# Feature transform with 256-column matmuls, and the rest queries as one weight block ahead of the small transpose

## The chip, the core and the metric

The kernel runs on one core of one Trainium2 chip. The metric is device time in microseconds (us) of one execution; the time of a kernel is the median of its runs. A profiled execution gives the trace, and its own time is used where rows of the trace are added up.

## What is computed

Two layers of an encoder over 1040 positions (16 learned meta tokens and 1024 inputs) with 1024 channels. Each layer reads one RMS-normed input through a combined projection, and three groups of heads work on its parts. Cut to what the change touches:

```python
def fourier_mix(f_in, fourier_w):          # 4 heads of 64 channels
    y = fft2(x, axes=(position, channel), norm="ortho").real
    return einsum('blhc,hcd->blhd', y, fourier_w)

def attend(qb):                            # 4 heads, 128 nope + 64 rope channels
    s = einsum('bqhd,bkhd->bhqk', qb, k) * scale
    return einsum('bhqk,bkhd->bqhd', softmax(s), v)

h = h + concat[fourier * silu(g_f), pool * silu(g_p), attention * silu(g_a)] @ w_out[l]
```

All arithmetic is to float32 accuracy: an operand is split into a rounded high part and a low part that holds the difference (`hilo`, L75: ScalarE writes the high part, VectorE subtracts), and a product takes three matmuls, high by high, high by low and low by high (`mm3`, L70).

## The kernel before, in words

The program is written stage by stage for TensorE, and a scheduler fixes the order of the instructions on each engine when the program is built. Each engine then works its own list in that order and waits where a buffer or an operand is not ready. Tiles come from pools with a fixed number of buffers: `slab` (36 buffers of 128x1056, SBUF), `mid` (10 buffers, SBUF), and in PSUM six banks with tag `mm` and two with tag `t`. A new tile takes a buffer as soon as the last reader of the tile that held it is done; until then its first writer waits, and with it all that stands behind that writer on its engine.

**Fourier group** (`dft_z` L498, `dft_y` L541, four passes `ty` per layer in the order 0, 2, 1, 3, between the matmuls of the gate projection of the attention group). `mc` holds the feature transform joined with `fourier_w`: four 128x128 matrices (cosine or sine, channel block j), each as a high and a low part. In `dft_z`, a row block `c` of the folded input (two full blocks; in every second pass a third of 80 rows, `fr`, that POOL puts together) is the stationary operand and `mc` streams past it. For each j there is one `mm3` of 128 columns into a `t` bank (L529), so six matmuls for a row block: `ah` by `mc` high, `ah` by `mc` low, `al` by `mc` high. ScalarE and VectorE then split the bank into `zt` (L532) or `ze` (L536, L537). `dft_y` takes `zt` as weights and streams the sine and cosine tables `dt` (262 columns), which POOL's queue loads into `mid` buffers (L506, L508).

**Attention** (L888 to L922). There are 16 groups `gi` per layer (4 heads by 4 blocks of 256 queries). A group has two tiles of 128 queries; `scores` (L705) fills three `mm` banks of 348, 348 and 344 keys, VectorE takes their maxima (L718), ScalarE the exponentials with a sum (L765, `soft` L760), VectorE scales (L773). `transposes` (L776) of the group before turns the probabilities for `values` (L811): steps kp 0 to 3 are four full transposes into a `t` bank (L802), then split by `hilo` into `pth` and `ptl`; step kp 4 is the small transpose of the last 16 keys (`rm`, L784), split into `pr`. `values` runs one group later still, into one `mm` bank (24 matmuls of 256 columns and two short ones).

**Rest queries.** In layer 0 the 1040 queries leave 16 over. `scores_rest` (L723) takes the 16 of all four heads as 64 rows: POOL writes their high parts, low parts and rope parts into `q3h` and `q3l`, blocks of 64 columns with zeros elsewhere (L725 to L732). For each of three key ranges 14 matmuls fill 64 rows of a bank: an `mm3` for each head and two for rope (L739 to L741). VectorE takes the maximum from PSUM (L742), and `soft` reads the bank. This is called in group 2, after `transposes(prev, (2, 3, 4))` and after `soft` of the second tile (L911 to L915).

Of the kernel before, what the change touches and what calls it, by code (L numbers as in the profile page):

```python
# [21 lines left out]
HEADS = 4  # L22
# [10 lines left out]
def fp(ap):  # L33
    return ap.bitcast(F32)
# [3 lines left out]
def hymba_encoder(ctx: ExitStack, tc: tile.TileContext, ht, win, wkr, vecs, fw, pw, wuq, wuk, wuv,  # L38
                  wout, cos_t, sin_t, dft_t, feat_t, fix_t, out):
    nc = tc.nc  # L40
# [23 lines left out]
    def bank(tag="mm"):  # L64
        return psum.tile([P, 512], F32, tag=tag, name=nm(tag), bufs=NMM if tag == "mm" else 8 - NMM)

    def mm(o, a, b, first, last):
        nc.tensor.matmul(o, a, b, start=first, stop=last)  # L68

    def mm3(o, wh, wl, xh, xl, first, last):  # L70
        mm(o, wh, xh, first, False)
        mm(o, wh, xl, False, False)
        mm(o, wl, xh, False, last)

    def hilo(hi, lo, src):  # L75
        nc.scalar.copy(hi, src)  # L76
        nc.vector.tensor_tensor(lo, src, fp(hi), ALU.subtract)  # L77
# [135 lines left out]
    for i in range(2):  # L213
        kind, src, k, m = jobs[i]
# [12 lines left out]
    for k in range(KC):  # L227
        h = slab("h")
# [36 lines left out]
    for l in range(DEPTH):  # L265
# [66 lines left out]
        s = add_square(add_square(None, zk[0], L), zk[1], L)  # L332
# [147 lines left out]
        nc.sync.dma_start(fwr, fw[l].rearrange("j p c -> p j c"))  # L480
        feat = mid("feat", [P, 2, P], F32)
        nc.sync.dma_start(feat, feat_t)
        mc = slab("mc", F32R, (P, 2, 4, P))
        b = bank("t")
        for part in range(2):
            for j in range(2):
                nc.tensor.matmul(b[:, (2 * part + j) * P:(2 * part + j + 1) * P], feat[:, part, :], fwr[:, j, :],
                                 start=True, stop=True)
        hilo(mc[:, 0], mc[:, 1], b.rearrange("p (a c) -> p a c", a=4))
        del fwr, feat  # L490
        FG.append(tile_now(scaled_tile(CQ, off, fn=AF.Silu)))
        Y = [slab("y0"), slab("y1")]
# [5 lines left out]
        def dft_z(ty):  # L498
            tabs, zs = [], []
            for c in range(3):  # L500
                rows = slice(0, P if c < 2 else 80)
                t = mid("dt", [P, 2, NF])
                if l == 0 and ty == 0:
                    nc.gpsimd.tensor_copy(t[rows, 0, 0:1], er[rows, 0:1])
                if c < 2:
                    nc.gpsimd.dma_start(t, dft_t[ty, c])  # L506
                else:
                    nc.gpsimd.dma_start(t[rows, 0, :], dft_t[ty, c, 0:80, 0, :])  # L508
                tabs.append(t)
            kind = ty // 2  # L510
            if ty % 2 == 0:
                fr = mid("fr", [P, 2, 2, 80])
                nc.gpsimd.memset(fp(fr), 0.0)
                for j in range(2):
                    for i in range(2):
                        for r in (0, 32, 64):
                            nc.gpsimd.tensor_copy(fr[:, j, i, r:r + 10].rearrange("p (a c) -> p a c", a=2),
                                                  fp(FH[j][i][:, ty:ty + 2, 256:261]))
            for c in range(2 + (ty % 2 == 0)):
                m = P if c < 2 else 80  # L520
                b = bank("t")
                for j in range(2):
                    if c < 2:
                        r = slice(P * c, P * c + P)
                        ah, al = FH[j][0][:, ty, r], FH[j][1][:, ty, r]
                    else:
                        ah, al = fr[:, j, 0, :], fr[:, j, 1, :]
                    mi = 2 * kind + j
                    mm3(b[0:m, j * P:(j + 1) * P], ah, al, mc[:, 0, mi, :], mc[:, 1, mi, :], True, True)  # L529
                if c < 2:  # L530
                    z = mid("zt", [P, 2, 256])
                    hilo(z[:, 0, :], z[:, 1, :], b[:, 0:256])  # L532
                    zs.append(z)
                else:
                    z = mid("ze", [80, 256])
                    nc.scalar.copy(z, b[0:80, 0:256])  # L536
                    nc.vector.tensor_tensor(z[32:64, :], b[32:64, 0:256], fp(z[32:64, :]), ALU.subtract)  # L537
                    ends[kind] = z
            return tabs, zs

        def dft_y(ty, tz, cc):  # L541
# [43 lines left out]
        zq, s = [], None  # L585
        for t in range(3):
            z = tile_now(raw_tile(CQ, off))
            s = add_square(s, z, NQ)
# [4 lines left out]
            if t == 1:  # L593
                KRH, KRL = slab("krh", F32R), slab("krl", F32R)
# [59 lines left out]
        parts = []  # L654
# [65 lines left out]
            nc.vector.tensor_reduce(mx[:, 3:4], mx[:, 0:3], AX.X, ALU.max, negate=True)  # L720
            return P, mx, bs

        def scores_rest():  # L723

            q3h, q3l = mid("q3h", [P, 5, 64]), mid("q3l", [P, 4, 64])  # L725
            nc.gpsimd.memset(fp(q3h), 0.0)
            nc.gpsimd.memset(fp(q3l), 0.0)
            for h in range(HEADS):
                r = slice(16 * h, 16 * h + 16)
                nc.gpsimd.tensor_copy(q3h[:, h, r], fp(QN[h][0][:, 1024:1040]))  # L730
                nc.gpsimd.tensor_copy(q3l[:, h, r], fp(QN[h][1][:, 1024:1040]))
                nc.gpsimd.tensor_copy(q3h[:, 4, r], fp(QR[h][:, 1024:1040]))  # L732
            mx = small("mx", [P, 4])
            bs = []
            for i, (c0, n) in enumerate(FULL):
                ks = slice(c0, c0 + n)
                o = bank()[0:64, :n]
                for h in range(HEADS):
                    mm3(o, q3h[:, h, :], q3l[:, h, :], KN[h][0][:, ks], KN[h][1][:, ks], h == 0, False)  # L739
                mm(o, q3h[:, 4, :], KRH[:, ks], False, False)  # L740
                mm(o, q3h[:, 4, :], KRL[:, ks], False, True)  # L741
                nc.vector.tensor_reduce(mx[0:64, i:i + 1], o, AX.X, ALU.max)  # L742
                bs.append(o)
            nc.vector.tensor_reduce(mx[0:64, 3:4], mx[0:64, 0:3], AX.X, ALU.max, negate=True)
            return 64, mx, bs

        def transposes_rest(p):
            t3 = sm_pool.tile([P, 2, 8, 64], F32R, tag="t3", name=nm("t3"), bufs=1)
# [9 lines left out]
            return t3, r3  # L758

        def soft(sc, rem=None):  # L760
            m, mx, bs = sc
            p = slab("p")
            sums = small("sums", [P, 4])
            for i, (c0, n) in enumerate(FULL):
                nc.scalar.activation(p[0:m, c0:c0 + n], bs[i], AF.Exp, bias=mx[0:m, 3:4],  # L765
                                     accum_out=sums[0:m, i:i + 1])
            nc.vector.tensor_reduce(sums[0:m, 3:4], sums[0:m, 0:3], AX.X, ALU.add)
            nc.vector.reciprocal(sums[0:m, 3:4], sums[0:m, 3:4])
            if rem is None:
                nc.vector.tensor_scalar(p[0:m, :L], p[0:m, :L], sums[0:m, 3:4], None, ALU.mult)  # L770
            else:
                nc.scalar.activation(rem, p[:, 1024:1040], AF.Copy, scale=sums[:, 3:4])
                nc.vector.tensor_scalar(p[:, :1024], p[:, :1024], sums[:, 3:4], None, ALU.mult)  # L773
            return p
# [114 lines left out]
        for gi, (h, g, tiles) in enumerate(groups):  # L889
            if g == 0:  # L890
                gate[h] = slab("gate")
                nc.sync.dma_start(gate[h][:, :NQ], gate_d[l][h, :, :NQ])
            cur = (h, g, small("rm", [P, 32], 3), [], [None] * 5)
            sc = scores(h, tiles[0])
            if gi == 0:
                cur[3].append(soft(sc, cur[2][:, 0:16]))
                QN.append(nope(CQN, 3, CQ, "qn"))
            if pend is not None:
                values(pend)
                if pend[1] == 3:  # L900
                    gate.pop(pend[0])
            if gi > 0:
                cur[3].append(soft(sc, cur[2][:, 0:16]))
            if prev is not None:
                transposes(prev, (0, 1))
            sc = scores(h, tiles[1])
            if gi == 0:
                QN.append(nope(CQN, 3, CQ, "qn"))
                del CQN
            if prev is not None:  # L910
                transposes(prev, (2, 3, 4))  # L911
                prev[3].clear()
            cur[3].append(soft(sc, cur[2][:, 16:32]))
            if l == 0 and gi == 2:
                rest = soft(scores_rest())  # L915
# [165 lines left out]
```

## Time and profile before

| what | value |
|---|---|
| median of 3 runs | 1073.85 us (1073.82 to 1075.18) |
| the profiled execution | 1075.23 us |
| its span, first to last instruction | 1073.5 us |
| TensorE (PE) busy | 1054.4 us, 98%, 6774 matmuls |
| TensorE weight loads (PEld) | 998.4 us, 93% |
| VectorE (DVE) busy | 700.0 us, 65% |
| ScalarE (ACT) busy | 512.8 us, 48% |
| GpSimd (POOL) busy | 96.1 us, 9% |
| mean granted clock of TensorE | 0.995 |

Matmuls are pipelined: a row of 0.32 us is the latency of one, and the next one starts well before it ends. What a matmul costs in a stream is the distance from its start to the start of the next. A bracket at the end of a row of a timeline is the idle time of the engine before that instruction, and what ended it.

### The profile page before, as it was taken

How to read it: one execution, taken by the hardware profiler on the slowest of the kernel's cores; microseconds unless marked ns; L12 is line 12 of the kernel's file. 1: busy time of each engine (PE TensorE's matmuls, PEld its weight loads, DVE VectorE, ACT ScalarE, POOL GpSimd, SP SyncE). 2: the span in 40 equal slices, each digit the busy share in tenths (PEclk: the TensorE clock that was granted, in tenths of full speed). 3: DMA queues.
4: the chain of work that ended last, by engine and by line, in shares of the span. 5: the costliest groups of instructions: out<-in, count | busy, mean ns of one | idle time of the engine just before them, and what ended most of it. 6: DMA issues, size and time to landing. Idle time of an engine off the chain costs nothing.

```text
span 1073.5 us, 17783 instructions
## 1 busy us (share of the span) xinstructions
PE 1054.4 (98%) x6774; PEld 998.4 (93%) x6774; DVE 700.0 (65%) x1422; ACT 512.8 (48%) x1203; POOL 96.1 (9%) x223
## 2 busy tenths in 40 slices
PE   8999999999999999999999999999999999999996
PEld 7999999999998899999999898888888899999995
DVE  6677543547577588888645765334575678888755
ACT  7532232353155467677534312323431566777674
POOL 0100020000000000001430001210000000000055
PEclk9999999999999999999999999999999999999998
DMA  6331123126550000013644111241274500001513
GB/s 234 93 120 40 49 84 116 51 73 228 196 144 1 21 17 5 22 40 119 195 133 118 51 49 40 83 125 45 84 261 156 128 1 21 21 20 41 168 40 118
DMA packets 52373, 95.26 MB, mean 89 GB/s; under 512 B 5312, under 2 KB 27584, under 8 KB 52288
## 3 DMA queue, kind: packets, MB, share of 16 engines
q1 hardware_dynamic: 49216, 89.17, 25.5%
q0 software_dynamic: 3072, 4.96, 1.9%
q8 instruction: 53, 0.87, 0.3%
q14 instruction: 32, 0.26, 0.1%
HBM read 66.62 MB, written 21.14 MB: 82 GB/s over the span
## 4 chain that ended last, share of the span: by engine, by line
PE 91%; DVE 4%; DMA 2%; ACT 1%; issue 1%; SPq 0%; DVEq 0%; ACTq 0%
PE mm L68 85%; PE t L802 4%; PE t L68 2%; DVE mx L718 1%; DMA pwr<-in_pw 1%; ACT p L765 1%; DVE ptl L77 1%; DMA h<-in_ht 1%; DVE wp L77 0%; DMA hq<-part_d 0%; DVE p L773 0%; DVE om L829 0%; PE t L784 0%; DMA wraw<-in_win 0%; DVE wlo L77 0%
## 5 line engine op out<-in xcount | busy, mean ns | idle before, releaser
L68 PE MATMUL mm<-hh,whi 128*128 128x348 f32 (+2 forms) x728 | 246.0, 340 | 1.3 <-ACT hh L202 0.7
L68 PE MATMUL mm<-hl,whi 128*128 128x348 f32 (+2 forms) x728 | 245.7, 339 | 0.4 <-DVE hl L203 0.4
L68 PE MATMUL mm<-hh,wlo 128*128 128x348 f32 (+2 forms) x728 | 245.9, 339 | 0.2 <-DVE wlo L77 0.2
L76 ACT CAST whi<-wraw 128x512 fp32r<-128x512 f32 (+3 forms) x110 | 64.5, 586 | 239.5 <-PE mm L68 233.1
L77 DVE TENSOR_TENSOR wlo<-wraw,whi 128x512 fp32r<-128x512 f32 (+3 forms) x110 | 70.8, 646 | 131.0 <-PE mm L68 77.8
L68 PEld LDWEIGHTS mm<-hh,whi 128*128 128x128 f32 x728 | 136.5, 188 | 9.6 <-ACT hh L202 1.3
L68 PEld LDWEIGHTS mm<-hl,whi 128*128 128x128 f32 x728 | 136.8, 188 | 8.3 <-DVE hl L203 0.7
L68 PEld LDWEIGHTS mm<-hh,wlo 128*128 128x128 f32 x728 | 136.8, 188 | 7.6 <-DVE wlo L77 0.5
L765 ACT ACTIVATE p<-mm,mx 128x348 f32<-128x348 f32 (+2 forms) x195 | 105.6, 555 | 13.3 <-DVE mx L720 12.7
L68 PE MATMUL mm<-pth,v 128*128 128x256 f32 (+1 forms) x512 | 106.6, 284 | 1.8 <-ACT p L765 0.8
L76 ACT CAST pth<-t 128x512 fp32r<-128x512 f32 x128 | 75.8, 593 | 67.8 <-PE t L802 67.2
L718 DVE TENSOR_REDUCE mx<-mm 128x1 f32<-128x348 f32 (+1 forms) x192 | 95.5, 513 | 15.4 <-PE mm L68 14.7
L68 PE MATMUL mm<-mah,wp 128*128 128x256 f32 (+1 forms) x512 | 94.1, 283 | 0.0
L77 DVE TENSOR_TENSOR ptl<-t,pth 128x512 fp32r<-128x512 f32 x128 | 86.3, 684 | 8.4 <-ACT pth L76 7.4
L68 PEld LDWEIGHTS mm<-pth,v 128*128 128x128 f32 x512 | 83.2, 189 | 3.4 <-ACT pth L76 1.2
L68 PEld LDWEIGHTS mm<-mah,wp 128*128 128x128 f32 x512 | 79.6, 189 | 0.1
L68 PE MATMUL mm<-ptl,v 128*128 128x256 f32 (+1 forms) x256 | 78.9, 308 | 0.0
L802 PE MATMUL t<-ident,p 128*128 128x128 f32 x512 | 76.8, 275 | 0.5 <-DVE ptl L77 0.2
L68 PE MATMUL mm<-mal,wp 128*128 128x256 f32 (+1 forms) x256 | 72.6, 284 | 0.0
L868 POOL TENSOR_TENSOR ssq<-ssq,sq 128x256 f32<-128x256 f32 (+1 forms) x49 | 37.6, 768 | 346.1 <-ACT sq L863 344.1
L68 PE MATMUL mm<-knh,qnh 128*128 128x348 f32 (+1 forms) x192 | 66.0, 344 | 0.5
L68 PE MATMUL mm<-knl,qnh 128*128 128x348 f32 (+1 forms) x192 | 61.9, 322 | 0.0
(237 smaller groups left out, 2190.7 us busy)
## 6 DMA issues: line engine op xcount, KB each, us to landing
wraw<-in_win SPq DMA_DIRECT2D x66, 256.0 KB, 2.6
wraw<-in_wout SPq DMA_DIRECT2D x32, 256.0 KB, 2.8
hq<-part_d SPq DMA_DIRECT2D x12, 512.0 KB, 5.4
dt<-in_dft_t POOLq DMA_DIRECT2D x16, 262.0 KB, 3.1
hres<-in_ht SPq DMA_DIRECT2D x8, 520.0 KB, 6.5
part_d<-hres SPq DMA_DIRECT2D x8, 520.0 KB, 3.7
hres<-h_d SPq DMA_DIRECT2D x8, 512.0 KB, 6.4
part_d<-hres SPq DMA_DIRECT2D x8, 512.0 KB, 3.9
```

Source lines behind the costliest of these rows:

```text
L68: nc.tensor.matmul(o, a, b, start=first, stop=last)
L76: nc.scalar.copy(hi, src)
L77: nc.vector.tensor_tensor(lo, src, fp(hi), ALU.subtract)
L718: nc.vector.tensor_reduce(mx[:, i:i + 1], o, AX.X, ALU.max)
L765: nc.scalar.activation(p[0:m, c0:c0 + n], bs[i], AF.Exp, bias=mx[0:m, 3:4], accum_out=sums[0:m, i:i + 1])
L802: nc.tensor.transpose(bv[:, a, t * P:(t + 1) * P], ps[t][:, kc * P:(kc + 1) * P], ident)
L868: eng.tensor_tensor(ssn[:, cs_], ssn[:, cs_], q[:, :n], ALU.add)
```

## The change

It has two parts. In the feature transform, `mc` is laid out with the high and the low part of each matrix side by side, so that `ah` meets both in one matmul of 256 columns; `al` meets the high part alone in one of 128. A bank then holds the main sum in one half of each j and the product with the low part in the other half, and they are added when the bank is read: ScalarE copies the main sum rounded (high part), VectorE subtracts it from the main sum into a new `mid` tile `zd`, and VectorE adds the other half into the low part. That is one instruction and one `mid` tile more for each row block.

For the rest queries, `q3` holds the high and the low parts of a head as one weight block of 128 columns (64 and 64). A key range takes four matmuls with that block against the high keys (128 output rows), four of 64 rows against the low keys and two for rope: ten in place of fourteen. ScalarE copies rows 64 to 127 to a slab `s3`, VectorE adds rows 0 to 63, and VectorE takes the maximum from `s3`; the exponentials are then written in place. The blocks are built in group 0 (`rest_parts`), and in group 2 the scores of the rest come after `soft` of the second tile and ahead of the small transpose (kp 4).

```diff
-        mc = slab("mc", F32R, (P, 2, 4, P))
+        mc = slab("mc", F32R, (P, 4, 2, P))
...
-        hilo(mc[:, 0], mc[:, 1], b.rearrange("p (a c) -> p a c", a=4))
+        hilo(mc[:, :, 0, :], mc[:, :, 1, :], b.rearrange("p (a c) -> p a c", a=4))
...
                     mi = 2 * kind + j
-                    mm3(b[0:m, j * P:(j + 1) * P], ah, al, mc[:, 0, mi, :], mc[:, 1, mi, :], True, True)
+                    r = slice(256 * j, 256 * j + 256)
+                    mm(b[0:m, r], ah, mc[:, mi, :, :].rearrange("p a c -> p (a c)"), True, False)
+                    mm(b[0:m, 256 * j:256 * j + P], al, mc[:, mi, 0, :], False, True)
+                bv = b.rearrange("p (j a c) -> p a j c", j=2, a=2)
                 if c < 2:
                     z = mid("zt", [P, 2, 256])
-                    hilo(z[:, 0, :], z[:, 1, :], b[:, 0:256])
                     zs.append(z)
+                    hi, lo, rows = z[:, 0, :], z[:, 1, :], slice(0, P)
                 else:
                     z = mid("ze", [80, 256])
-                    nc.scalar.copy(z, b[0:80, 0:256])
-                    nc.vector.tensor_tensor(z[32:64, :], b[32:64, 0:256], fp(z[32:64, :]), ALU.subtract)
                     ends[kind] = z
+                    hi, lo, rows = z, z[32:64, :], slice(32, 64)
...
+                own = hi[rows]
+                nc.scalar.copy(hi, bv[0:m, 0])
+                d = mid("zd", [P, 2, P], F32)[rows]
+                nc.vector.tensor_tensor(d, bv[rows, 0], fp(own), ALU.subtract)
+                nc.vector.tensor_tensor(lo, bv[rows, 1], d, ALU.add)
...
-        def scores_rest():
+        def rest_parts():
+            q3, qr3 = mid("q3", [P, 4, P]), mid("qr3", [P, 64])
+            nc.gpsimd.memset(fp(q3), 0.0)
             for h in range(HEADS):
                 r = slice(16 * h, 16 * h + 16)
+                nc.gpsimd.tensor_copy(q3[:, h, 16 * h:16 * h + 16], fp(QN[h][0][:, 1024:1040]))
+                nc.gpsimd.tensor_copy(q3[:, h, 64 + 16 * h:80 + 16 * h], fp(QN[h][1][:, 1024:1040]))
+                nc.gpsimd.tensor_copy(qr3[:, r], fp(QR[h][:, 1024:1040]))
+            return q3, qr3
+
+        def scores_rest(parts):
...
+            s3, bs = slab("s3"), []
             for i, (c0, n) in enumerate(FULL):
                 ks = slice(c0, c0 + n)
-                o = bank()[0:64, :n]
+                b = bank()
+                o, s = b[0:64, :n], s3[0:64, ks]
                 for h in range(HEADS):
-                    mm3(o, q3h[:, h, :], q3l[:, h, :], KN[h][0][:, ks], KN[h][1][:, ks], h == 0, False)
-                mm(o, q3h[:, 4, :], KRH[:, ks], False, False)
-                mm(o, q3h[:, 4, :], KRL[:, ks], False, True)
-                nc.vector.tensor_reduce(mx[0:64, i:i + 1], o, AX.X, ALU.max)
-                bs.append(o)
+                    if h == 0:
+                        mm(b[:, :n], q3[:, h, :], KN[h][0][:, ks], True, False)
+                    mm(o, q3[:, h, 0:64], KN[h][1][:, ks], False, False)
+                mm(o, qr3, KRH[:, ks], False, False)
+                mm(o, qr3, KRL[:, ks], False, False)
+                for h in range(1, HEADS):
+                    mm(b[:, :n], q3[:, h, :], KN[h][0][:, ks], False, h == HEADS - 1)
+                nc.scalar.copy(s, b[64:128, :n])
+                nc.vector.tensor_tensor(s, o, s, ALU.add)
+                nc.vector.tensor_reduce(mx[0:64, i:i + 1], s, AX.X, ALU.max)
+                bs.append(s)
...
             if prev is not None:
-                transposes(prev, (2, 3, 4))
+                transposes(prev, (2, 3))
+            if l == 0 and gi == 2:
+                cur[3].append(soft(sc, cur[2][:, 16:32]))
+                sc = scores_rest(rest)
+                transposes(prev, (4,))
+                rest = soft(sc)
+            else:
...
```

How the built lists of the engines stand to each other: outside the four passes of the Fourier group (both layers) and groups 2 to 6 of layer 0's attention, TensorE's list is the same in both programs.

**TensorE, one row block of the feature transform in layer 0** (`t_` is the bank, `fah` and `fal` the input's parts, two numbers for j = 0 and 1). Before, ended by the next matmul of the projection:

```order
L68 MATMUL t_1585<-mc_1292,fah_1269 128x128 x2
L68 MATMUL t_1585<-mc_1292,fal_1270 128x128
L68 MATMUL t_1585<-mc_1292,fah_1284 128x128 x2
L68 MATMUL t_1585<-mc_1292,fal_1285 128x128
L68 MATMUL mm_1615<-hh_131,whi_1453 128x348
```

With the change:

```order
L68 MATMUL t_1585<-mc_1292,fah_1269 128x256
L68 MATMUL t_1585<-mc_1292,fal_1270 128x128
L68 MATMUL t_1585<-mc_1292,fah_1284 128x256
L68 MATMUL t_1585<-mc_1292,fal_1285 128x128
L68 MATMUL mm_1615<-hl_150,whi_1453 128x348
```

Six matmuls became four, each with a weight load of its own; the place among the projection's matmuls moved by a few.

**TensorE, group 2 of layer 0, from the last full transposes on** (`mm_3650`, `mm_3666` and `mm_3682` are the banks of the rest's three key ranges, `mm_3709` is the next group's scores). Before:

```order
L802 MATMUL t_3609<-ident,p_3410 128x128
L802 MATMUL t_3609<-ident,p_3484 128x128
L784 MATMUL t_3618<-ident,rm_3386 32x128
L68 MATMUL mm_3650<-knh_2314,q3h_3633 64x348
L68 MATMUL mm_3650<-knl_2315,q3h_3633 64x348
L68 MATMUL mm_3666<-knh_2314,q3h_3633 64x348
L68 MATMUL mm_3666<-knl_2315,q3h_3633 64x348
L68 MATMUL mm_3682<-knh_2314,q3h_3633 64x344
L68 MATMUL mm_3682<-knl_2315,q3h_3633 64x344
L68 MATMUL mm_3709<-knh_2314,qnh_3155 128x348
```

With the change, the first key range (bank `mm_3644`; the other two follow, with the same ten):

```order
L824 MATMUL t_3624<-ident,p_3425 128x128
L824 MATMUL t_3624<-ident,p_3499 128x128
L68 MATMUL mm_3644<-knh_2314,q_549_3377 128x348
L68 MATMUL mm_3644<-knl_2315,q_549_3377 64x348
L68 MATMUL mm_3644<-knl_2350,q_549_3377 64x348
L68 MATMUL mm_3644<-knl_2385,q_549_3377 64x348
L68 MATMUL mm_3644<-knl_2420,q_549_3377 64x348
L68 MATMUL mm_3644<-krh_2216,qr_550_3378 64x348
L68 MATMUL mm_3644<-krl_2217,qr_550_3378 64x348
L68 MATMUL mm_3644<-knh_2349,q_549_3377 128x348
L68 MATMUL mm_3644<-knh_2384,q_549_3377 128x348
L68 MATMUL mm_3644<-knh_2419,q_549_3377 128x348
```

and further on, behind all thirty of them:

```order
L68 MATMUL mm_3672<-knh_2419,q_549_3377 128x344
L68 MATMUL mm_3702<-knh_2314,qnh_3155 128x348
L68 MATMUL mm_3702<-knl_2315,qnh_3155 128x348
L68 MATMUL mm_3702<-knh_2314,qnl_3156 128x348
L68 MATMUL mm_3702<-krh_2216,qr_3002 128x348
L68 MATMUL mm_3702<-krl_2217,qr_3002 128x348
L68 MATMUL mm_3709<-knh_2314,qnh_3155 128x348
L806 MATMUL t_3687<-ident,rm_3401 32x128
L68 MATMUL mm_3709<-knl_2315,qnh_3155 128x348
```

The small transpose stood right behind the eight full ones; it now stands behind thirty matmuls of the rest and six of the next scores. Before, all but six matmuls of the rest came after the fifteen of the next scores.

**VectorE, the row blocks of the first pass.** Before:

```order
L299 TENSOR_TENSOR u_1396<-mm_1450,y_384 128x348
L77 TENSOR_TENSOR zt_1427<-t_1420,zt_1427 128x256
L77 TENSOR_TENSOR zt_1437<-t_1430,zt_1437 128x256
L299 TENSOR_TENSOR u_1396<-mm_1451,y_384 128x348
L537 TENSOR_TENSOR ze_1447<-t_1440,ze_1447 32x256
```

With the change:

```order
L299 TENSOR_TENSOR u_1396<-mm_1450,y_384 128x348
L547 TENSOR_TENSOR zd_1427<-t_1420,zt_1425 128x256
L547 TENSOR_TENSOR zd_1437<-t_1430,zt_1435 128x256
L548 TENSOR_TENSOR zt_1425<-t_1420,zd_1427 128x256
L548 TENSOR_TENSOR zt_1435<-t_1430,zd_1437 128x256
L299 TENSOR_TENSOR u_1396<-mm_1451,y_384 128x348
```

Each row block has a second instruction on VectorE (20 in both layers), and the bank is free after the second.

## Rows read from the trace of the kernel before

**Rows 1.** The page: busy us (share of the span) and instructions by engine.
```profile
PE 1054.4 (98%) x6774; PEld 998.4 (93%) x6774; DVE 700.0 (65%) x1422; ACT 512.8 (48%) x1203; POOL 96.1 (9%) x223
```

**Rows 2.** Waits of PE: engine and line waited for, us in total, times, longest.
```profile
PE t L784 <- DVE ptl L77: 2.7, 2, 2.3
```

**Rows 3.** Timeline of PE, layer 0, group 2: start us, us, what, count.
```profile
345.44 1.10 PE L802 MATMUL t<-ident,p 128*128 128x128 f32 x8
348.85 0.28 PE L784 MATMUL t<-ident,rm 128*32 128x128 f32 x1 [2.31 <-DVE ptl L77]
...
349.29 0.49 PE L68 MATMUL mm<-knh,q3h 128*64 128x348 f32 x1
...
352.48 0.42 PE L68 MATMUL mm<-knh,qnl 128*128 128x348 f32 x1
352.73 0.32 PE L68 MATMUL mm<-krh,qr 128*128 128x348 f32 x1
352.89 0.32 PE L68 MATMUL mm<-krl,qr 128*128 128x348 f32 x1
```

**Rows 4.** Timelines of ACT and of DVE in group 2.
```profile
349.14 0.63 ACT L76 CAST pth<-t 128x512 fp32r<-128x512 f32 x1
...
348.11 0.69 DVE L77 TENSOR_TENSOR ptl<-t,pth 128x512 fp32r<-128x512 f32 x1
...
350.26 0.69 DVE L77 TENSOR_TENSOR ptl<-t,pth 128x512 fp32r<-128x512 f32 x1
```

**Rows 5.** Window: from:to us, length, busy of PE, PEld, DVE, ACT, POOL; PEclk, DMA.
```profile
348.95:352.48 3.53, 3.53 (x15) 3.28 (x15) 1.96 (x5) 1.42 (x7) 0.00 (x0) 0.54 0.00 0
```

**Rows 6.** Timeline of PE, one row block of the feature transform.
```profile
150.49 0.33 PE L68 MATMUL t<-mc,fah 128*128 128x128 f32 x2
150.66 0.27 PE L68 MATMUL t<-mc,fal 128*128 128x128 f32 x1
150.77 0.39 PE L68 MATMUL t<-mc,fah 128*128 128x128 f32 x2
...
151.10 0.37 PE L68 MATMUL mm<-hh,whi 128*128 128x348 f32 x1
```

**Rows 7.** Timeline of PE, table matmuls and a row block of 80.
```profile
148.08 0.52 PE L68 MATMUL mm<-dt,zt 128*128 128x262 f32 x3
148.44 0.58 PE L68 MATMUL t<-mc,fr 128*80 128x128 f32 x6
148.86 0.46 PE L68 MATMUL mm<-dt,zt 128*128 128x262 f32 x2
```

**Rows 8.** Groups of PE by form: count, busy us, mean ns, idle before.
```profile
L68 PE MATMUL t<-mc,fah 128*128 128x128 f32 x64 | 10.9, 264 | 0.0
```

**Rows 9.** Tile `t` in layer 0's four passes, and a window there.
```profile
L77 DVE TENSOR_TENSOR zt<-t,zt x8: 414/424/425, 145.1 to 182.3; 128x256 fp32r<-128x256 f32 x8
...
166.00:171.00 5.00, 5.00 (x37) 5.00 (x36) 3.67 (x10) 2.71 (x6) 0.55 (x1) 1.00 0.49 139
```

**Rows 10.** DMA issues: KB each, median us to landing.
```profile
dt<-in_dft_t POOLq DMA_DIRECT2D x16, 262.0 KB, 3.1
```

**Rows 11.** Timeline of PE, eight transposes with no wait behind them.
```profile
399.21 1.12 PE L802 MATMUL t<-ident,p 128*128 128x128 f32 x8
400.08 0.41 PE L68 MATMUL mm<-knh,qnh 128*128 128x348 f32 x1
```

**Rows 12.** Timeline of ACT, group 2, the first tile's first exponential.
```profile
345.31 0.56 ACT L765 ACTIVATE p<-mm,mx 128x348 f32<-128x348 f32 x1
```

**Rows 13.** Timeline of PE, the values of the group behind the rest.
```profile
359.51 1.04 PE L802 MATMUL t<-ident,p 128*128 128x128 f32 x8
361.37 0.39 PE L68 MATMUL mm<-pth,v 128*128 128x256 f32 x1 [0.83 <-ACT p L765]
```

**Rows 14.** Lines 351 and 352: ns min/median/max, starts, forms.
```profile
L351 ACT COPY ktmp<-mm x6: 443/446/447, 46.0 to 576.7; 64x348 f32<-64x348 f32 x4, 64x344 f32<-64x344 f32 x2
...
L352 DVE TENSOR_TENSOR kz<-mm,ktmp x6: 495/505/512, 48.5 to 577.2; 64x348 f32<-64x348 f32 x4, 64x344 f32<-64x344 f32 x2
```

More of the change, by code (lines that the diff above doesn't have):

```diff
@@ L528, in dft_z @@
                     mi = 2 * kind + j
-                    mm3(b[0:m, j * P:(j + 1) * P], ah, al, mc[:, 0, mi, :], mc[:, 1, mi, :], True, True)
+                    r = slice(256 * j, 256 * j + 256)
+                    mm(b[0:m, r], ah, mc[:, mi, :, :].rearrange("p a c -> p (a c)"), True, False)
+                    mm(b[0:m, 256 * j:256 * j + P], al, mc[:, mi, 0, :], False, True)
+                bv = b.rearrange("p (j a c) -> p a j c", j=2, a=2)
                 if c < 2:
                     z = mid("zt", [P, 2, 256])
-                    hilo(z[:, 0, :], z[:, 1, :], b[:, 0:256])
                     zs.append(z)
+                    hi, lo, rows = z[:, 0, :], z[:, 1, :], slice(0, P)
                 else:
                     z = mid("ze", [80, 256])
-                    nc.scalar.copy(z, b[0:80, 0:256])
-                    nc.vector.tensor_tensor(z[32:64, :], b[32:64, 0:256], fp(z[32:64, :]), ALU.subtract)
                     ends[kind] = z
+                    hi, lo, rows = z, z[32:64, :], slice(32, 64)
+                hi = hi.rearrange("p (j c) -> p j c", j=2)
+                lo = lo.rearrange("p (j c) -> p j c", j=2)
+                own = hi[rows]
[3 more added lines that the diff above has]
+                nc.vector.tensor_tensor(lo, bv[rows, 1], d, ALU.add)
             return tabs, zs
@@ L721, in scores @@
             return P, mx, bs
-        def scores_rest():
-            q3h, q3l = mid("q3h", [P, 5, 64]), mid("q3l", [P, 4, 64])
-            nc.gpsimd.memset(fp(q3h), 0.0)
-            nc.gpsimd.memset(fp(q3l), 0.0)
+        def rest_parts():
+            q3, qr3 = mid("q3", [P, 4, P]), mid("qr3", [P, 64])
+            nc.gpsimd.memset(fp(q3), 0.0)
             for h in range(HEADS):
                 r = slice(16 * h, 16 * h + 16)
-                nc.gpsimd.tensor_copy(q3h[:, h, r], fp(QN[h][0][:, 1024:1040]))
-                nc.gpsimd.tensor_copy(q3l[:, h, r], fp(QN[h][1][:, 1024:1040]))
-                nc.gpsimd.tensor_copy(q3h[:, 4, r], fp(QR[h][:, 1024:1040]))
+                nc.gpsimd.tensor_copy(q3[:, h, 16 * h:16 * h + 16], fp(QN[h][0][:, 1024:1040]))
+                nc.gpsimd.tensor_copy(q3[:, h, 64 + 16 * h:80 + 16 * h], fp(QN[h][1][:, 1024:1040]))
+                nc.gpsimd.tensor_copy(qr3[:, r], fp(QR[h][:, 1024:1040]))
+            return q3, qr3
@@ L733, in scores_rest @@
+        def scores_rest(parts):
+            q3, qr3 = parts
             mx = small("mx", [P, 4])
-            bs = []
+            s3, bs = slab("s3"), []
             for i, (c0, n) in enumerate(FULL):
                 ks = slice(c0, c0 + n)
-                o = bank()[0:64, :n]
+                b = bank()
+                o, s = b[0:64, :n], s3[0:64, ks]
                 for h in range(HEADS):
-                    mm3(o, q3h[:, h, :], q3l[:, h, :], KN[h][0][:, ks], KN[h][1][:, ks], h == 0, False)
-                mm(o, q3h[:, 4, :], KRH[:, ks], False, False)
-                mm(o, q3h[:, 4, :], KRL[:, ks], False, True)
-                nc.vector.tensor_reduce(mx[0:64, i:i + 1], o, AX.X, ALU.max)
-                bs.append(o)
+                    if h == 0:
[9 more added lines that the diff above has]
+                bs.append(s)
@@ L744, in scores_rest @@
             nc.vector.tensor_reduce(mx[0:64, 3:4], mx[0:64, 0:3], AX.X, ALU.max, negate=True)
-            return 64, mx, bs
+            return 64, mx, bs, s3
         def transposes_rest(p):
@@ L760, in soft @@
         def soft(sc, rem=None):
-            m, mx, bs = sc
-            p = slab("p")
+            m, mx, bs, *own = sc
+            p = own[0] if own else slab("p")
             sums = small("sums", [P, 4])
@@ L909, in hymba_encoder @@
                 del CQN
+                if l == 0:
+                    rest = rest_parts()
             if prev is not None:
-                transposes(prev, (2, 3, 4))
+                transposes(prev, (2, 3))
[5 more added lines that the diff above has]
+            else:
+                if prev is not None:
+                    transposes(prev, (4,))
+                cur[3].append(soft(sc, cur[2][:, 16:32]))
+            if prev is not None:
                 prev[3].clear()
-            cur[3].append(soft(sc, cur[2][:, 16:32]))
-            if l == 0 and gi == 2:
-                rest = soft(scores_rest())
             if l == 0 and gi == 3:
```

## The prediction

> **What bounds the kernel now.** I read the page first: TensorE is busy 1054.4 of 1073.5 us [rows 1], so nearly everything the kernel can gain lies on that engine, either as matmuls taken out or as its few idle stretches. The other engines count only where TensorE waits for them. The list of TensorE's waits comes next. Its largest entry is the small transpose (L784), which waits for VectorE's write of `ptl`: 2.7 us in all, 2.3 us in one place [rows 2]. The timeline shows that place. Eight full transposes start at 345.44, the small one at 348.85 [rows 3]. It needs one of two `t` banks, and that one is free when VectorE's `ptl` of 348.11 ends, near 348.8 [rows 4]. The scores of the rest stand behind it on TensorE and wait with it. After the gap, matmuls of 348 columns start 0.29 us apart, until 352.48; from there the distance is 0.16 us [rows 3]. The window says why: the granted clock is 0.54 in that stretch [rows 5], so most of it ran at 1.2 GHz in place of 2.4. Before the fall the engine had stood idle 2.3 us. So that wait costs twice, as a gap and as a slow stretch behind it.
>
> **The feature transform.** A row block takes six matmuls of 128 columns; the first starts at 150.49, the next matmul of the projection at 151.10, so 0.61 us [rows 6]. A run goes as two in 0.17 us, then 0.11 us for each [rows 6]: the first distance is 0.06 us, all others 0.11. Matmuls of 262 columns follow each other in 0.12 us [rows 7]. Twice the columns for nearly the same time means that the short ones are held up by something other than their columns. Each has a weight load of its own, and on 80-column weights the six take 0.42 us, 0.07 each [rows 7], so it is the load.
>
> Now four: 256, 128, 256, 128 columns. If only columns counted, it would be 0.12 + 0.06 + 0.12 + 0.06 = 0.36 us. If a short one still takes 0.11, it is 0.12 + 0.11 + 0.12 + 0.11 = 0.46. Four loads at 0.11 make 0.44, but the first is hidden behind the matmul ahead, as before; I take the middle, 0.40. The saving is 0.21 us for a row block (0.15 to 0.25). There are 64 `fah` matmuls, four to a row block, so 16 row blocks [rows 8]: 3.4 us (2.4 to 4.0). The four row blocks of 80 take 0.42 now, and 0.36 by the columns, since their loads are shorter: 0.2 us (0 to 0.3). Together **3.6 us** (2.4 to 4.3).
>
> What it adds runs beside TensorE: 20 more instructions on VectorE, at 0.42 us for 128x256 [rows 9] about 8 us in all. In the four passes of layer 0 the busiest 5 us that I looked at have VectorE at 3.67 [rows 9], and TensorE has matmuls of the projection in between. A `t` bank is now held one such instruction longer. In the new list the next user of the same bank is at least some 20 matmuls away, over 2 us; copy, subtraction and addition take some 1.3 us at 0.42 each. The high part is first used 2 us or more after its matmuls. So I cost it at nothing; without that cover it is 0.42 us of TensorE idle for a row block. `mc` is one tile as before, and its split is the same two instructions.
>
> The new `zd` tiles take `mid` buffers, so the table loads of POOL's queue can start later: in the new list the second pass's first table waits for the last `fr` matmul of the first, and its user is some 75 matmuls of 0.16 us further, about 12 us. A table takes 3.1 us to land [rows 10]. Cost nothing; what it would be if not, is a rival below.
>
> **The rest's matmuls.** Ten in place of fourteen for each of three ranges, all of 348 or 344 columns: 12 fewer at 0.16 us [rows 3], **1.9 us**. The weight blocks grow from 64 to 128 columns, but the 128-column blocks of the ordinary scores already follow each other in 0.16 us [rows 3]. So the wider blocks cost nothing. The Trainium skill, "TensorE: Matmul & The Clock Gate", section "LDWEIGHTS (loading the stationary operand)", speaks against this part: a load's time goes with the columns of the weights, so a block of 128 takes twice as long to load as one of 64. By its formula the 12 wide blocks would load 0.05 us longer each, an estimate of 0.6 us less gain if loads lay open; the trace's 0.16 us with 128 columns says that they are hidden, and the sum goes by that.
>
> **The order in group 2.** The small transpose goes behind 36 matmuls, 5.8 us at 0.16. Eight unobstructed transposes take 0.87 us to the next start [rows 11], so the ones of 345.44 are through at 346.31, and the gap to 348.85 is **2.5 us**. The rest's first matmul can start there: its bank comes free with the first tile's first exponential, which ends before 346 [rows 12]; `q3` has been built since group 0, on POOL, in `mid` buffers that no one waits for. The small transpose then comes near 352, long after its bank is free (348.8). Without the gap the clock should not fall: 11 distances of 0.29 us between 349.29 and 352.48 are 3.19 us, at 0.16 they are 1.76, so **1.4 us** [rows 3].
>
> Next, what is late then. Before, the values of group 1 start at 361.37, while the eight transposes of 359.51 are through at 360.38 [rows 11, 13]: **1.0 us** of waiting. They need a bank of the rest, and that one is free only after the rest's exponential, which needs the maxima of all three ranges. Now VectorE's addition frees it. I follow that new chain. ScalarE's queue is through its cast at 349.8 [rows 4] and copies range one in 0.45 us [rows 14], to 350.2; VectorE is through at 351.0 [rows 4] and adds in 0.5 us [rows 14], to 351.5. The values come after 30 + 15 matmuls, the small transpose and four full ones, so near 346.3 + 45 x 0.16 + 0.1 + 0.4 = 354.0. That is 2.5 us of slack. The third range's matmuls end at 351.1, its copy and addition by 352.4, and the exponentials follow near 355.7, since some seven maxima and writes of about 0.45 us stand between on VectorE. The next group's exponentials queue behind them on ScalarE and free the banks that the scores of group 4 need near 360.7, at about that time. So this place is tight, and I charge **0.4 us** for one late bank, with 0 to 1.4 us as bounds: nothing, or as much as the values lost before and 0.4 more.
>
> **Sum.** 3.6 + 1.9 + 2.5 + 1.4 + 1.0 - 0.4 = 10.0 us. The profiled execution took 1075.23 us, 1.7 more than its span; 1065.2 after the change. The median of the runs lies 1.4 lower, at 1073.85, so I expect **1063.8 us**. By the bounds the gain is 7.8 to 11.1 us, 1062.7 to 1066.1. Later waits of group 4 may also go, or lengthen, with the new list; I allow 1.5 us to either side.
>
> **Rivals.**
> - *The wait moves.* The rest's new evacuation has six more instructions than before on ScalarE and VectorE, and the exponentials of the next group stand behind them. If TensorE then stops for a bank as long as it did, with the clock falling again, the 2.5, 1.4 and 1.0 us come back, and 3.6 + 1.9 - 0.4 = 5.1 us remain: 1068.8. For it: the place is tight by my own count. Against it: both engines have little to do after 351 [rows 5], where VectorE is busy 1.96 of 3.53 us.
> - *The load does not count.* If a matmul of 256 columns with this operand layout takes as long as two of 128, the first part gives nothing: 1067.4. Against it: 262 columns in 0.12 us [rows 7].
> - *Slower, through the tables.* `zd` takes `mid` buffers in each pass, and a table that lands late stops TensorE at its first table matmul. Priced by the gap above, a stop that the clock follows costs 2.5 + 1.4 = 3.9 us. There are eight passes. It decides from four late passes: 15.6 us lost against 10.0 gained, 1079.5. For it: the buffers are ten, and nearly all in use. Against it: 12 us of matmuls stand between, and a table needs 3.1 us and its issue.
>
> **How the numbers follow.** My sum has a chance of 0.78, the moved wait 0.10, the load 0.08, the tables 0.04. The moved wait and the main case's bounds set the range: 1061.2 to 1068.9 leaves out the tables and the tails, under 2 in 10. A measurement of this kernel can tell 0.2% from no change, 2.1 us: faster means under 1071.7, slower over 1076.0. All cases but the tables are faster; a mix of the tables with a moved wait can come out even. So 0.94 faster, 0.03 same, 0.03 slower.
>
> **What would show it.** In the new profile: row blocks of four matmuls in about 0.40 us; no wait of L784's successor, and the small transpose right between the scores; PEclk at 1.00 from group 2 on, and a mean clock above 0.995; the values of group 1 some 7 us earlier in their stretch (361.37 before, plus what the passes gave); 52 matmuls fewer. I am wrong if TensorE shows a new idle stretch over 1 us in groups 2 to 5 or before a table matmul, or if the row blocks take 0.6 us still.

## The result and the profile after

| | before | after |
|---|---|---|
| median, runs side by side | 1074.55 us (1073.82 to 1075.76) | 1062.91 us (1062.28 to 1064.45) |
| ratio, 95% interval | | 0.9893 (0.9883 to 0.9904) |
| the profiled execution, its span | 1075.23, 1073.5 us | 1062.90, 1061.1 us |
| one stretch of TensorE: from the wait for `wlo` near 22 us to the wait for `om` near 390 us | 376.15 us | 366.11 us |

The stretch of the last row (22.16 to 398.31 in before, 22.59 to 388.70 in after) is used for all runs. It holds layer 0 from the end of the start-up to group 6 of its attention, so all of the rest's part and half of the feature transform, and it leaves out the start, where executions differ by 0.4 us and more.

The page of after, busy time by engine, answers to [rows 1]: 52 matmuls fewer, 8.3 us less of TensorE's time.

```profile
PE 1046.1 (99%) x6722; PEld 991.5 (93%) x6722; DVE 708.4 (67%) x1445; ACT 514.3 (48%) x1206; POOL 97.3 (9%) x222
```

Waits of TensorE in after (us in total, times, longest), against [rows 2]: the small transpose, now L806, waits 0.3 us once, at 466.01, and not in group 2.

```profile
PE t L806 <- DVE ptl L77: 0.3, 1, 0.3
```

TensorE's timeline in after, group 2 (start, us, what, count), against [rows 3, 13]. The rest starts 0.86 us after the first of the eight transposes; the small transpose stands between the scores; the values of group 1 follow four transposes at 352.43. No row has a bracket, so nothing waits there.

```profile
343.95 1.11 PE L824 MATMUL t<-ident,p 128*128 128x128 f32 x8
344.81 0.40 PE L68 MATMUL mm<-knh,q 128*128 128x348 f32 x1
345.05 0.78 PE L68 MATMUL mm<-knl,q 128*64 128x348 f32 x4
...
350.39 0.32 PE L68 MATMUL mm<-knh,qnh 128*128 128x348 f32 x1
350.55 0.27 PE L806 MATMUL t<-ident,rm 128*32 128x128 f32 x1
350.57 0.41 PE L68 MATMUL mm<-knl,qnh 128*128 128x348 f32 x1
...
352.07 0.60 PE L824 MATMUL t<-ident,p 128*128 128x128 f32 x4
352.43 0.37 PE L68 MATMUL mm<-pth,v 128*128 128x256 f32 x1
```

Windows of after (from:to, length, busy of PE, PEld, DVE, ACT, POOL, then PEclk), against [rows 5]: the granted clock stays at 1.00.

```profile
343.95:347.50 3.55, 3.55 (x26) 3.20 (x25) 2.98 (x8) 3.55 (x14) 0.00 (x0) 1.00 0.00 0
347.50:351.00 3.50, 3.50 (x25) 3.31 (x24) 3.22 (x8) 2.37 (x9) 0.00 (x0) 1.00 0.00 0
```

TensorE's timeline in after, a row block of 80 and one of 128, against [rows 6, 7]: 0.37 us in place of 0.42, and 0.40 (151.08 to 151.48) in place of 0.61.

```profile
149.68 0.53 PE L68 MATMUL t<-mc,fr 128*80 128x256 f32 x4
150.05 1.19 PE L68 MATMUL mm<-dt,zt 128*128 128x262 f32 x8
151.08 0.28 PE L68 MATMUL t<-mc,fah 128*128 128x256 f32 x1
151.19 0.22 PE L68 MATMUL t<-mc,fal 128*128 128x128 f32 x1
151.25 0.33 PE L68 MATMUL t<-mc,fah 128*128 128x256 f32 x1
151.42 0.22 PE L68 MATMUL t<-mc,fal 128*128 128x128 f32 x1
151.48 0.37 PE L68 MATMUL mm<-hl,whi 128*128 128x348 f32 x1
151.69 0.32 PE L68 MATMUL mm<-hh,wlo 128*128 128x348 f32 x1
```

The last two rows show more: the 348-column matmul behind the block has 0.21 us to the next start, where 0.16 is usual. That belongs to the block too; e5 below says why.

### The profile page after: what moved, and what is told of

Its sections match the earlier page's. It is cut to its first block, busy times and chain, and to the rows that moved or that the text cites. A ratio compares the mean times of both kernels' runs of the same rounds, so it can differ in the third digit from the quotient of the medians.

```text
span 1061.1 us, 17711 instructions
## 1 busy us (share of the span) xinstructions
PE 1046.1 (99%) x6722; PEld 991.5 (93%) x6722; DVE 708.4 (67%) x1445; ACT 514.3 (48%) x1206; POOL 97.3 (9%) x222
## 4 chain that ended last, share of the span: by engine, by line
PE 91%; DVE 4%; DMA 2%; ACT 1%; issue 1%; SPq 0%; DVEq 0%; ACTq 0%
PE mm L68 85%; PE t L824 5%; PE t L68 1%; DMA pwr<-in_pw 1%; DVE mx L728 1%; DMA h<-in_ht 1%; DVE hq L905 1%; DVE ptl L77 1%; DVE wp L77 0%; DVE om L851 0%; DVE p L795 0%; ACT sq L885 0%; PE t L806 0%; ACT p L787 0%; DMA wraw<-in_win 0%
## 5 line engine op out<-in xcount | busy, mean ns | idle before, releaser
L68 PE MATMUL mm<-hl,whi 128*128 128x348 f32 (+1 forms) x728 | 245.4, 338 | 0.0
L787 ACT ACTIVATE p<-mm,mx 128x348 f32<-128x348 f32 (+1 forms) x192 | 103.7, 554 | 10.0 <-DVE mx L730 9.4
L68 PE MATMUL mm<-krh,qr 128*128 128x348 f32 (+2 forms) x195 | 62.7, 322 | 0.0
```

## The experiments

All of them at a glance; differences are to the kernel before, by the ratio and, in the stretch, by the trace.

| run | median us | ratio (95%) | by the ratio | stretch, us | by the stretch |
|---|---|---|---|---|---|
| after | 1062.91 | 0.9893 (0.9883 to 0.9904) | -11.5 | 366.11 | -10.04 |
| e1 feature alone | 1071.48 | 0.9966 (0.9954 to 0.9977) | -3.7 | 374.21 | -1.94 |
| e2 blocks early | 1070.14 | 0.9956 (0.9943 to 0.9969) | -4.7 | 370.99 | -5.16 |
| e3 rest alone | 1067.42 | 0.9929 (0.9915 to 0.9943) | -7.6 | 368.12 | -8.03 |
| e4 six matmuls | 1067.96 | 0.9937 (0.9924 to 0.9950) | -6.8 | 368.12 | -8.03 |
| e5 low part by 256 | 1063.47 | 0.9897 (0.9883 to 0.9910) | -11.1 | 366.34 | -9.81 |
| e6 blocks late | 1070.14 | 0.9957 (0.9945 to 0.9970) | -4.6 | 373.12 | -3.03 |
| e8 early, slab | 1069.30 | 0.9948 (0.9935 to 0.9960) | -5.6 | 369.99 | -6.16 |

e7 and e9 change the loop of the attention itself and stand below the table: 1069.56 us (0.9953, 0.9939 to 0.9966) and 1073.93 us (0.9993, 0.9984 to 1.0002).

**e1 and e3, the two parts apart.** e1 is before with the feature transform's part of the change alone (layout of `mc`, four matmuls, three-step evacuation); e3 is before with the rest's part alone.

> The kernel before with the new feature transform alone (layout of mc, four matmuls for a row block, evacuation in three steps); the rest queries stay as they were. Theory: the part gives what its row blocks give in the trace of after, 11.65 - 8.14 = 3.5 us, so 3.5 us faster than before (allow 3.0 to 4.0), with the wait of the small transpose, the slow clock behind it and the values' wait all still there. Rival: the added subtraction and the zd tiles give part of it back, under 2.5 us faster.

> The whole change to the rest queries alone (stacked blocks, built in group 0, new order); the feature transform as before. Theory: 1.9 + 2.5 + 1.4 + 1.0 and the later waits of groups 3 to 5, 1.3, make 8.1 us faster than before (allow 7.3 to 9.0), and with the feature transform alone it adds up to the whole change. Rival: the later waits went because of the feature part, 6.8 us faster here and more than the parts together in the whole.

Both came as expected, and they add up: 1.94 + 8.03 = 9.97 us in the stretch, where the whole change has 10.04. In e1 the small transpose still waits 2.30 us, with 11 matmuls at half clock further on, and the values wait 0.91 us, where before has 0.83. So the feature transform touches none of the rest's waits. TensorE's timeline in e1:

```profile
347.12 0.28 PE L794 MATMUL t<-ident,rm 128*32 128x128 f32 x1 [2.30 <-DVE ptl L77]
```

**e4, the evacuation.** The changed kernel, with the matmul of 256 cut in two:

```diff
-  mm(b[0:m, r], ah, mc[:, mi, :, :].rearrange("p a c -> p (a c)"), True, False)
+  mm(b[0:m, 256 * j + P:256 * j + 256], ah, mc[:, mi, 1, :], True, True)
+  mm(b[0:m, 256 * j:256 * j + P], ah, mc[:, mi, 0, :], True, False)
```

> The changed kernel with the matmul of 256 columns cut into two of 128 (high by low into the other half, then high by high): six matmuls and six weight loads for a row block as before, but the new layout, the evacuation in three steps and the zd tiles. Theory: it loses all that the feature transform gave, 3.5 us slower than the changed kernel and equal to the change to the rest alone within 0.5 us, since the added evacuation costs nothing. Rival: the evacuation costs something, then it is slower than the rest alone by that, up to 0.42 us for each of 20 row blocks, 8 us.

In the stretch it takes 368.12 us, as e3 does to the last digit, and its row blocks take 0.61 us again. The copy, the subtraction, the addition and the `zd` tiles cost nothing there. The medians differ by 0.5 us, and to after by 5.0, where I had said 3.5. Behind the stretch, e4 has a wait of 0.74 us for a split of `pth` at 492.89, and e5 one of 0.76 at the same place, 490.51; e3 and after have none over 0.15 us there. e1, with no change to the rest, has one of 0.82 at 488.12, where before has 0.27. It comes and goes with small shifts in time, and no run ties it to a part.

**e5, columns or loads.** The changed kernel, with as many matmuls and more columns:

```diff
-  mm(b[0:m, 256 * j:256 * j + P], al, mc[:, mi, 0, :], False, True)
+  mm(b[0:m, r], al, mc[:, mi, :, :].rearrange("p a c -> p (a c)"), False, True)
```

> The changed kernel, where the low part of the input also meets both parts of the matrix in 256 columns (low by low is added to the result, which the reference's rounding does not need): the number of matmuls and of weight loads stays, 128 columns more for each of 40 matmuls. In the trace of after a short matmul of 128 columns takes 0.06 us to the next start and the one behind it 0.17 in place of 0.12. Theory (columns and loads overlap, the longer of the two counts): a row block goes from 0.41 to 4 x 0.12 = 0.47 us, one of 80 rows from 0.36 to 0.47; 16 x 0.06 + 4 x 0.11 = 1.4 us slower than the changed kernel. Rival (loads alone count): 0 to 0.3 us slower.

TensorE's timeline in e5, a row block:

```profile
150.41 0.28 PE L68 MATMUL t<-mc,fah 128*128 128x256 f32 x1
150.53 0.28 PE L68 MATMUL t<-mc,fal 128*128 128x256 f32 x1
150.65 0.28 PE L68 MATMUL t<-mc,fah 128*128 128x256 f32 x1
150.77 0.28 PE L68 MATMUL t<-mc,fal 128*128 128x256 f32 x1
150.89 0.32 PE L68 MATMUL mm<-hl,whi 128*128 128x348 f32 x1
151.04 0.32 PE L68 MATMUL mm<-hh,wlo 128*128 128x348 f32 x1
```

The block takes 0.48 us, as the theory has it, but the kernel hardly pays for it: the stretch is 0.2 us longer, in place of the 0.7 that layer 0's half of 1.4 would be (the rival's half is 0 to 0.15), and the medians lie within their intervals. The rows say where it goes. Behind a matmul of 256 columns the next starts after 0.12 us, and the 348-column one has 0.15. Behind a short one the next matmul is late by 0.05, and the last of these delays falls outside the block. With that delay a block of after takes 0.61 us from its first start to the second matmul behind it (151.08 to 151.69), the one of e5 0.63. The short matmul hides only 0.06 us of the next load, and what is left of the load shows one place later. So loads decide, close to the rival's reading: 2 loads fewer for a row block.

**e2 and e6, what moved the rest.** With only the written order of group 2 put back (kp 4 ahead of the rest, blocks still in group 0), the built program is the changed kernel's own, instruction by instruction on all engines, so there was nothing to run. The written order moves nothing, and two kernels tell what does. e2 is before with the old blocks written early; e6 is after with the blocks written late:

```diff
 e2, against before
             if gi == 0:
                 QN.append(nope(CQN, 3, CQ, "qn"))
                 del CQN
+                if l == 0:
+                    rest = rest_parts()
...
-                rest = soft(scores_rest())
+                rest = soft(scores_rest(rest))
 e6, against after
-                if l == 0:
-                    rest = rest_parts()
...
-                sc = scores_rest(rest)
+                sc = scores_rest(rest_parts())
```

> The kernel before with one thing changed: the rest's blocks, in their old form (q3h, q3l, fourteen matmuls for a key range, maxima and exponentials from PSUM), are written by POOL in group 0 in place of group 2. The written order in group 2 stays: small transpose, soft, rest. Theory A (a scheduler places by readiness, so the build is what moves the rest ahead of the small transpose): gap 2.5 us and slow clock 1.4 us go, the values' 1.0 us goes too because the rest's exponentials can come some 6 us earlier, 4.9 us faster than before, up to 6.2 if the later waits of groups 3 to 5 (1.3 us) go with them. Rival B (the written order counts): no difference from before. Rival C (banks held until the exponentials keep stopping the values and the next scores): 3.9 us faster, with a wait for a bank of about 1 us in groups 3 to 5.

> The changed kernel with one thing undone: the stacked blocks are written in group 2, just ahead of the rest's scores, in place of group 0. The written order (rest ahead of the small transpose) and the feature transform stay. Theory (the time of the build decides where a scheduler puts the rest): the built list has the small transpose right behind the full ones again, and behind it eight transposes that need group 2's own second tile, so the gap of 2.5 us is back and longer by about 1.3, with 1.4 us or more of slow clock behind it: 4 to 6 us slower than the changed kernel. Rival (the written order decides): no difference from the changed kernel.

TensorE's timeline in e2. The rest starts right behind the full transposes although the small one is written first, and the values of group 1 (356.35) no longer wait. Two later delays stay: 0.48 us of idle time at 375.75, and 0.45 us from there to the next start, at 376.20, where e8 below has 0.20:

```profile
345.51 1.11 PE L805 MATMUL t<-ident,p 128*128 128x128 f32 x8
346.38 0.40 PE L68 MATMUL mm<-knh,q3h 128*64 128x348 f32 x1
...
352.12 0.27 PE L787 MATMUL t<-ident,rm 128*32 128x128 f32 x1
...
355.56 1.03 PE L805 MATMUL t<-ident,p 128*128 128x128 f32 x8
356.35 0.37 PE L68 MATMUL mm<-pth,v 128*128 128x256 f32 x1
...
374.24 1.04 PE L805 MATMUL t<-ident,p 128*128 128x128 f32 x8
375.75 0.36 PE L68 MATMUL mm<-pth,v 128*128 128x272 f32 x1 [0.48 <-ACT pth L76]
376.20 0.43 PE L68 MATMUL mm<-knh,qnh 128*128 128x348 f32 x1
```

TensorE's timeline in e6. The small transpose is back behind the full ones, and so are its 2.31 us; the next eight transposes wait another 1.87:

```profile
347.11 0.28 PE L806 MATMUL t<-ident,rm 128*32 128x128 f32 x1 [2.31 <-DVE ptl L77]
349.26 1.97 PE L824 MATMUL t<-ident,p 128*128 128x128 f32 x8 [1.87 <-DVE ptl L77]
...
351.32 0.49 PE L68 MATMUL mm<-knl,q 128*64 128x348 f32 x1
351.61 0.49 PE L68 MATMUL mm<-knh,q 128*128 128x348 f32 x1
```

Windows of e6 behind it (columns as above): the granted clock is at half for 5 us.

```profile
349.30:351.30 2.00, 2.00 (x9) 1.96 (x10) 0.22 (x1) 0.00 (x0) 0.00 (x0) 0.50 0.00 0
351.30:354.30 3.00, 3.00 (x12) 2.85 (x11) 0.00 (x0) 0.00 (x0) 0.00 (x0) 0.50 0.00 0
```

Theory A holds on both sides. e2 gains 5.16 us in the stretch: 2.5 for the gap, 1.4 for the clock, 1.0 for the values, 0.3 elsewhere; its granted clock stays at 1.00 from 345 to 356. e6 loses 7.0 against after, where I had said 4 to 6: the two waits of 2.31 and 1.87, and an estimate of 2.5 for 5 us of matmuls at half clock, make most of it. On the chip POOL has written e6's blocks by 343.8 us (its last copy starts at 343.60 and takes 0.20), before the gap begins near 344.8, so the rest could have started. What holds it back is the list that was fixed when the program was built.

**e8, the later waits.** e2 with the rest's scores copied to a slab `s3`, in which `soft` then writes the exponentials:

```diff
...
-                nc.vector.tensor_reduce(mx[0:64, i:i + 1], o, AX.X, ALU.max)
-                bs.append(o)
+                nc.scalar.copy(s, o)
+                nc.vector.tensor_reduce(mx[0:64, i:i + 1], s, AX.X, ALU.max)
+                bs.append(s)
...
```

> The kernel of e2 (old blocks, written in group 0) with one thing more from the change: ScalarE copies the rest's scores from PSUM to a slab, maxima and exponentials work on that slab in place, so each of the three banks is free after its copy. The fourteen matmuls for a key range stay. In e2 two waits of groups 4 and 5 were left (0.64 and 0.33 us, values for pth, scores for p); with the stacked blocks they were gone. Theory (the early release of the banks took them away): they go here too, 1 us faster than e2. Rival (it was the stacked blocks' twelve matmuls fewer and the list that a scheduler makes from them, which puts the rest's transposes earlier): the waits stay, no difference from e2 within 0.5 us.

TensorE's timeline in e8, at the place of e2's two delays:

```profile
374.90 0.60 PE L806 MATMUL t<-ident,p 128*128 128x128 f32 x4
375.53 0.36 PE L68 MATMUL mm<-pth,v 128*128 128x272 f32 x1
375.73 0.32 PE L68 MATMUL mm<-knh,qnh 128*128 128x348 f32 x1
```

The stretch is 1.00 us shorter than e2's. The copy takes the two delays away; the twelve matmuls are not needed for it. The list changed with it (four transposes ahead of the values in place of eight), so whether the banks alone do it, or the list that their release makes, is not told apart. From e2 to e3 the stretch gains 2.87 us, which is this 1.0 and 1.9 for twelve matmuls of 0.16.

**e7 and e9, a step further.** The last 16 keys take two short matmuls in each group (L846, L849). I made them one of 256 columns, with the mask on the probabilities:

```diff
 e7 and e9, values
-            mm(b[:, 0:P], vr[0][:, vs], pt[4][0], False, False)
...
-            mm(b[:, P:256], vr[1][:, vs], pt[4][0], False, True)
+            mm(b[:, 0:256], vr[:, vs], pt[4][0], False, True)
 e7, evacuation, for each half t (o is its slice)
+                        nc.scalar.activation(pr[0:32, t * P:t * P + P], b[0:32, 0:P], AF.Copy,
+                                             scale=turn[0:32, t:t + 1])
...
+                        nc.vector.scalar_tensor_tensor(pr[32:64, o], b[0:32, 0:P], turn[0:32, t:t + 1],
+                                                       fp(pr[0:32, o]), ALU.mult, ALU.subtract)
 e9, evacuation as in after (into pu), then for each half t
+                        nc.gpsimd.tensor_scalar(pr[:, t * P:t * P + P], fp(pu), turn[0:96, t:t + 1], None, ALU.mult)
```

> The changed kernel with the same idea at one more place: the last 16 keys of a group's two tiles, which take two matmuls of 128 columns with two masked weight blocks in every group, take one of 256 columns with one block; the mask (turn) goes to the transposed probabilities, with one instruction more on ScalarE and one more on VectorE for each group. In the trace two of these matmuls take 0.17 us to the next start, one of 256 columns takes 0.12. Theory: 32 matmuls fewer, 32 x 0.05 = 1.7 us faster than the changed kernel. Rival (the longer evacuation of the small transpose holds its t bank and delays the next transposes): no gain, or up to 1 us slower.

> As e7 (one matmul of 256 columns for the last 16 keys), but ScalarE and VectorE evacuate the small transpose as in the changed kernel, and POOL puts the two masked halves together from SBUF, two instructions a group. e7 lost 6.6 us against the changed kernel in waits of the values for pth and p. Theory (what cost it was the new order of the lists: with 32 matmuls fewer values stand nearer behind the full transposes whose split they need): the same waits, 3 to 7 us slower than the changed kernel. Rival (the longer evacuation on ScalarE and VectorE cost it): no such waits, 1.7 us faster than the changed kernel.

Neither gains: 6.7 and 11.0 us slower than after by the medians, with 32 matmuls fewer. TensorE's timeline in e7 shows the values right behind the transposes and a wait that after does not have:

```profile
361.24 0.60 PE L827 MATMUL t<-ident,p 128*128 128x128 f32 x4
361.79 0.27 PE L804 MATMUL t<-ident,rm 128*32 128x128 f32 x1
363.54 0.39 PE L68 MATMUL mm<-pth,v 128*128 128x256 f32 x1 [1.48 <-ACT p L785]
```

and TensorE's timeline in e9 a set of twelve transposes with one matmul between, where after has four, two matmuls, four, then scores. There are two `t` banks, and the third set waits for one:

```profile
428.46 1.04 PE L825 MATMUL t<-ident,p 128*128 128x128 f32 x8
429.45 0.38 PE L68 MATMUL mm<-pr,vr 96*128 96x256 f32 x1
430.51 0.66 PE L825 MATMUL t<-ident,p 128*128 128x128 f32 x4 [0.68 <-DVE ptl L77]
```

e9 keeps the evacuation of after on ScalarE and VectorE and loses more than e7, so a longer evacuation there is not the cause of e9's loss; and none of its waits of TensorE over 0.15 us ends with one of POOL's instructions. Of my two readings the new order is the one that is left, but it is not shown: e9's waits are others than e7's, its loss is larger than the 3 to 7 us that I expected, and no run kept the order while it took the matmuls out. What 32 matmuls fewer are worth stays open, and so does the share of e7's longer evacuation.

## Why the prediction was right, step by step

- **Feature transform, 3.6 us.** e1: 3.7 by the ratio. The row blocks take 11.65 us in before and 8.14 in after. With what the matmul behind each run of them takes beyond its usual distance (0.16 us for 348 columns, 0.12 for 262, 0.23 for 512) it is 12.85 and 9.13, so 3.7. The 0.40 us for a row block was right (0.40 to 0.43), though I took it as a middle of two pictures; e5 shows that it is the load throughout. The Trainium skill, "TensorE: Matmul & The Clock Gate", section "LDWEIGHTS (loading the stationary operand)", gives a load's time by the columns of the weights: an estimate of 0.107 us for 128 and 0.067 for 80. The trace agrees, with 0.11 and 0.07 between short matmuls [rows 6, 7].
- **Evacuation, `zd`, tables at nothing.** Right: e4 and e3 have the same stretch.
- **Rest's matmuls, 1.9 us.** Right: e2 to e3 less e8's share. The wide blocks follow each other in 0.16 us. So the longer load of the Trainium skill's rule above stays hidden here.
- **Gap 2.5 and clock 1.4.** Right in size: e2 takes both away, e1 has them, e6 has them and more. The cause was not told apart: I read it off the list and spoke of the order in group 2. It is the time at which the blocks are written; the written order does nothing.
- **Values' wait, 1.0.** Right in size, partly by luck: the reason that I gave is not the one that decides. I said that VectorE's addition frees the bank. In e2 there is no addition, the exponentials still free it, and the wait is gone all the same, because the whole chain comes earlier: the last of them starts at 355.18, the values at 356.35. What the early copy does remove is the later delays, 1.0 us (e8), which I had left in the allowance of 1.5.
- **The charge of 0.4.** The mis-sized term: no late bank, 0. VectorE and ScalarE had more room than I counted. The three additions are over by 351.2, the rest's exponentials by 356.1, and the scores of group 4 start at 359.39 with 0.15 us of delay. Rows of tile `s` in after (ns min/median/max, starts):

```profile
L763 DVE TENSOR_TENSOR s<-mm,s x3: 497/502/502, 349.4 to 350.6; 64x348 f32<-64x348 f32 x2, 64x344 f32<-64x344 f32 x1
...
L787 ACT ACTIVATE s<-s,mx x3: 567/571/587, 354.4 to 355.5; 64x348 f32<-64x348 f32 x2, 64x344 f32<-64x344 f32 x1
```

- **Rivals.** None came: in after no wait over 0.15 us stands in groups 2 to 5 or at a table matmul, and four matmuls do take 0.40 us.
- **Sum.** 10.0 by the terms, 11.6 by the medians. With what the runs gave it is 3.7 + 1.9 + 2.5 + 1.4 + 1.0, nothing charged, and 1.0 for the later delays: 11.5. The profiled executions lie 12.3 us apart; the other 0.8 no run ties to a part.

## What to carry to other kernels

Where a run of short matmuls takes as long as its weight loads, count the loads: cutting six to four took a block from 0.61 to 0.40 us, and 128 more columns on the short ones were nearly free. Where a scheduler fixes the order when the program is built, look at what it takes an operand's readiness from; writing small operands early moved the work, and reordering the calls did not. And taking a matmul out inside a tuned loop can cost more than it saves: e7 and e9 came with a new list, new waits and a loss. So compare the lists before counting the gain.

## What the runs showed that I had not expected

- A weight load that a short matmul does not hide shows up behind the block, on a matmul of another stage (0.21 us where 0.16 is usual). Sums that stop at the block miss it: e5's blocks grew by 1.29 us in all (9.43 against 8.14), its stretch by 0.2.
- The clock and idle time, in the same loop: after 2.3 us of idle TensorE the granted clock fell to 0.50, which is 1.2 GHz (before, e1, e6); after 1.48 us in e7 it stayed at 1.00, 2.4 GHz. Windows of TensorE in e7 (from:to, length, busy of PE, then PEclk), the idle stretch and the one behind it:

```profile
361.90:363.50 1.60, 0.16 (x1) 1.00 0.00 0
363.50:367.00 3.50, 3.46 (x30) 1.00 0.00 0
```
